# The down projection starts on the tokens' first half, operand sums are made in place, and layer normalization's reciprocals are pinned: one decoder layer in single precision

## The chip, the cores and the metric

The kernel runs on one core of a Trainium2 chip. The time is the device time of one execution in microseconds (us); for the kernel before it is the median of three runs, and the rows come from one further execution that the hardware profiler recorded. Engines: TensorE (PE) multiplies, VectorE (DVE), ScalarE (ACT) and GpSimd (POOL) do elementwise work, SyncE (SP) issues loads. POOL issues the DMAs that add to their destination.

## The reference, cut to what matters

One layer on 1024 tokens with 1024 channels, all in float32. The part that most of the change touches is the channel mixer's end:

```python
h = rmsnorm(x, g_ffn[i])
u = jnp.einsum("bsd,df->bsf", h, w_up[i])                      # 1024 -> 2 x 2816
f_gate = causal_dwconv(u[..., :D_FF], conv_f_w[i]) + conv_f_b[i]
f = jax.nn.gelu(f_gate, approximate=True) * u[..., D_FF:]
x = x + jnp.einsum("bsf,fd->bsd", f, w_down[i])                # 2816 -> 1024
pg = jax.nn.sigmoid(jnp.einsum("bsd,de->bse", rmsnorm(x, g_ple[i]), w_ple_gate[i]))
```

Before it stand an input projection (`w_in`, operand h), two convolution branches (one with a layer normalization over 512 channels), their merge, and an output projection; all are touched only through the operand sums and the normalization's two reciprocals.

## The kernel before

Channels lie on partitions (tiles of 128), tokens along the free dimension, 1024 of them in two halves `H0` and `H1` of 512. A float32 operand is held as two halves of its precision, `hi` (an ACT cast, L132) and `lo` (a DVE subtraction, L133), and one product of a weight block with an operand is three matmuls of 128x512 (hi·hi, hi·lo, lo·hi).

The large products are done in pairs: two row blocks of channels and the two token halves form a 2x2 block product, which class `Pair` (L607) computes with seven products m = 1 to 7 instead of eight. Products 1, 2 and 3 use operand rows as they are (`r1` and `r2` are the first token half of two feature tiles, `r3` the second half of the second tile); 4 to 7 use sums of them. `right_sums` (L583) makes these sums into two fresh tiles `t13` and `t24`, and `sum_halves` (L592) casts and subtracts them into hi and lo. Weight sums come from DMAs that add, issued on POOL (L244); `w_s` is a weight sum, `w_r` and `w_q` are plain weights.

The down projection works through 22 feature tiles in three chunks of 4, 4 and 3 rows (a row is a pair of tiles, k and 11+k). `f`, the product that the up projection left in DRAM (`f_d`), is loaded per chunk. A chunk has 28 steps (p, m): four pairs of output tiles p, seven products each; a step is 3 matmuls for each row, so 12 in the first two chunks and 9 in the last. The order of the steps, `dn_order`, is one list for all chunks: (0,1), (1,1), (0,2), (1,2), (0,6), ...; so four steps go by before the first sum is needed. `Rows.prepare` (L1108) is called after every step with the number of steps left before the chunk; it issues the loads (6 steps ahead for the first two rows of the first chunk, 3 for the other two, 14 elsewhere), the splits of plain operands and the sums (`Rows.sums`: rows 0 and 1 at two and one steps left, the others at none).

Results of the first two chunks are added to `x1_d` in DRAM by class `DnStore` (L1145) with DMAs of a full tile of 128x1024 (512 KB); the last chunk (`DnLast`, L1173) loads these tiles back (`x2`) and finishes them on DVE.

PE and SP run in the order of the code; the order on DVE, ACT and POOL is worked out by a scheduler, except for instructions given to `keep_in_program_order`. All three engines execute strictly in that order. `Loader` (L168) issues weights ahead by a distance in matmuls. Buffers are slots of one pool; the sums before take slots of their own.

## Time and profile before

| what | value |
|---|---|
| median of 3 runs | 1379.69 us (1376.6 to 1381.29) |
| profiled execution | 1382.37 us, of which the span (first to last instruction) is 1380.6 us |
| mean granted clock of TensorE | 0.972 |
| busy: PE / DVE / ACT / POOL | 1306.8 / 976.6 / 590.3 / 247.1 us |
| DMA moved | 245.25 MB |

The profile gives, for each stretch, how long an engine was busy and how many instructions it ran (x), the clock granted to TensorE (1.00 is 2.4 GHz, and 0.50 is 1.2 GHz), and the mean busy share of the 16 DMA engines. In full swing PE starts 90 matmuls of 128x512 in 20 us, so a stretch with fewer has lost the difference at 4.5 per us. PE's busy time hides this, since matmuls at the lower clock are busy for longer.

### The profile page before, as it was taken

The numbers are of one execution on the slowest core, as the hardware profiler recorded it, in microseconds if no ns is written. First come the engines' busy times: TensorE is split into PE (matmuls) and PEld (weight loads), VectorE is DVE, ScalarE is ACT, GpSimd is POOL, SyncE is SP. The second block draws the span as 40 slices with busy tenths as digits, with TensorE's granted clock in tenths as the row PEclk, the third lists the DMA queues.
The fourth block names the chain that finished last, engine by engine and source line by source line (L and its number), as shares of the span: only waits on it lengthen the run. The fifth ranks groups of instructions, "written<-read, shape, count | busy, mean of one in ns | idle before, by whom it ended". The sixth has DMA issues, their size and how long they took to land.

```text
span 1380.6 us, 15699 instructions
## 1 busy us (share of the span) xinstructions
PE 1306.8 (95%) x5798; PEld 1081.9 (78%) x5798; DVE 976.6 (71%) x1134; ACT 590.3 (43%) x814; POOL 247.1 (18%) x319
## 2 busy tenths in 40 slices
PE   9989999999999999899999999999976979989996
PEld 7768888788887788778888888888864867867996
DVE  7969999999448766486665566665676292588787
ACT  7443233233444334354344433444344262456554
POOL 1331221122100001122221222212112222320011
PEclk9989999999999999999999999999998999999998
DMA  9645696578676303597666776667666998994222
GB/s 339 183 119 125 179 237 159 142 200 212 196 272 233 122 24 130 163 205 189 177 167 175 198 186 172 174 168 192 187 181 162 272 222 204 211 234 153 76 91 73
DMA packets 102765, 245.25 MB, mean 178 GB/s; under 512 B 11680, under 2 KB 21664, under 8 KB 102688
## 3 DMA queue, kind: packets, MB, share of 16 engines
q1 hardware_dynamic: 61632, 148.81, 32.6%
q0 software_dynamic: 41056, 95.44, 32.1%
q8 instruction: 45, 0.74, 0.2%
q14 instruction: 32, 0.26, 0.1%
HBM read 173.42 MB, written 45.09 MB: 158 GB/s over the span
## 4 chain that ended last, share of the span: by engine, by line
PE 71%; DVE 14%; issue 8%; DMA 3%; ACT 2%; POOL 1%; SPq 0%; DVEq 0%; ACTq 0%; POOLq 0%
PE ps L629 50%; PE ps L155 14%; DVE acc L712 2%; PE ps L969 2%; PE ps L968 2%; PE ps L970 2%; DMA x_d<-dn 2%; DVE w_s_lo L133 1%; POOL s L244 1%; DMA f<-f_d 1%; DVE w_r_lo L133 1%; DVE x_raw L477 1%; DVE ft_lo L133 1%; DVE sc_cv L712 1%; DVE t L588 1%
## 5 line engine op out<-in xcount | busy, mean ns | idle before, releaser
L712 DVE SCALAR_TENSOR_TENSOR acc<-a,prm,acc 128x1023 f32<-128x1023 f32 (+14 forms) x120 | 151.8, 1265 | 1.7
L133 DVE TENSOR_TENSOR w_s_lo<-s,w_s_hi 128x1024 fp32r<-128x1024 f32 (+1 forms) x100 | 119.6, 1198 | 35.7 <-ACT w_s_hi L132 35.7
L244 POOL DMA_DIRECT2D s<-s x100 | 85.6, 856 | 298.2 <-DMA s<-s 126.0
L652 ACT COPY u<-ps 128x512 f32<-128x512 f32 x50 | 29.3, 586 | 202.3 <-PE ps L629 202.3
L132 ACT CAST w_s_hi<-s 128x1024 fp32r<-128x1024 f32 (+1 forms) x100 | 102.9, 1031 | 2.6 <-issue 1.7
L712 DVE SCALAR_TENSOR_TENSOR fg<-u_t,neg_f,fg 128x1023 f32<-128x1023 f32 (+1 forms) x44 | 56.5, 1283 | 28.3 <-ACT fg L706 27.6
L133 DVE TENSOR_TENSOR w_r_lo<-raw_r,w_r_hi 128x1024 fp32r<-128x1024 f32 (+1 forms) x50 | 59.8, 1197 | 17.2 <-ACT w_r_hi L132 17.2
L646 ACT COPY u<-ps 128x512 f32<-128x512 f32 x50 | 29.3, 586 | 92.4 <-PE ps L629 92.4
L629 PE MATMUL ps<-xgs_hi,w_s_lo 128*128 128x512 f32 x176 | 68.6, 390 | 0.0
L629 PE MATMUL ps<-xgs_lo,w_s_hi 128*128 128x512 f32 x176 | 68.5, 389 | 0.0
L629 PE MATMUL ps<-xgs_hi,w_s_hi 128*128 128x512 f32 x176 | 68.5, 389 | 0.0
L629 PE MATMUL ps<-xgp_hi,w_r_lo 128*128 128x512 f32 x176 | 68.5, 389 | 0.0
L629 PE MATMUL ps<-xgp_lo,w_r_hi 128*128 128x512 f32 x176 | 68.5, 389 | 0.0
L629 PE MATMUL ps<-xgp_hi,w_r_hi 128*128 128x512 f32 x176 | 68.5, 389 | 0.0
L639 ACT COPY ps<-ps 128x512 f32<-128x512 f32 x50 | 28.5, 571 | 87.6 <-PE ps L629 87.6
L1075 DVE TENSOR_TENSOR u_t<-ps,rstd 128x512 f32<-128x512 f32 x22 | 15.2, 691 | 69.7 <-PE ps L629 69.7
L155 PE MATMUL ps<-xp_hi,whi 128*128 128x448 f32 (+2 forms) x192 | 62.0, 323 | 1.9 <-DVE x L1201 1.9
L629 PE MATMUL ps<-xgq,w_s_hi 128*128 128x512 f32 x176 | 55.8, 399 | 7.2 <-DVE u_t L665 7.2
L155 PE MATMUL ps<-xp_lo,whi 128*128 128x448 f32 (+2 forms) x192 | 61.9, 323 | 0.0
L155 PE MATMUL ps<-xp_hi,wlo 128*128 128x448 f32 (+2 forms) x192 | 61.9, 323 | 0.0
L629 PE MATMUL ps<-xgt_hi,w_q 128*128 128x512 f32 x176 | 57.9, 390 | 0.7 <-ACT u L652 0.7
L629 PE MATMUL ps<-hss_hi,w_s_hi 128*128 128x512 f32 x128 | 50.9, 398 | 4.5 <-ACT w_s_hi L132 4.5
(297 smaller groups left out, 3718.7 us busy)
## 6 DMA issues: line engine op xcount, KB each, us to landing
s<-s POOLq DMA_DIRECT2D x92, 256.0 KB, 4.1
raw_r<-w_up SPq DMA_DIRECT2D x22, 512.0 KB, 4.7
s<-w_up SPq DMA_DIRECT2D x44, 256.0 KB, 3.0
s<-w_up SPq DMA_DIRECT2D x22, 512.0 KB, 5.8
s<-w_up POOLq DMA_DIRECT2D x44, 256.0 KB, 6.0
f_d<-v_t POOLq DMA_DIRECT2D x22, 512.0 KB, 5.9
f<-f_d SPq DMA_DIRECT2D x22, 512.0 KB, 9.8
s<-w_in SPq DMA_DIRECT2D x32, 256.0 KB, 3.2
```

The lines of the kernel that those rows point to most:

```text
L132: nc.scalar.copy(hi, src)
L133: nc.vector.tensor_sub(lo, src, f32(hi))
L155: nc.tensor.matmul(ps[:, :step], wt[:, b], xt[:, t : t + step], start=f, stop=l)
L244: nc.gpsimd.dma_start(dst, src, accum_op=ALU.add)
L629: nc.tensor.matmul(ps, wt[:, b], xt, start=f, stop=l, skip_group_check=True)
L639: nc.scalar.copy(self.b, self.a)
L646: nc.scalar.copy(self.e[:, H0], self.b)
L652: nc.scalar.copy(self.e[:, H1], self.b)
L712: nc.vector.scalar_tensor_tensor(dst[:, s:], src[:, : T - s], w(k), dst[:, s:], ALU.mult, ALU.add)
L968: nc.tensor.matmul(ps, whi[:, b], hi, start=first and k == ks[0], stop=False)
L969: nc.tensor.matmul(ps, whi[:, b], lo, start=False, stop=False)
L970: nc.tensor.matmul(ps, wlo[:, b], hi, start=False, stop=last and k == ks[-1])
```

## The change

It has five parts. (1) `dn_order` becomes a function of the chunk: the first eight steps of a chunk are now the products 1 and 2 of all four pairs, which need the first token half alone; the other steps follow in a new order. (2) `Rows` loads each pair of tiles by token halves (two DMAs of 256 KB into one tile, instead of one of 512 KB), and a table `STEPS` says at which step, counted from the chunk's first, each row is loaded, split and summed. (3) `right_sums` writes the sums over the tiles they are made of, for the input projection's h, the output projection's xg and for f. (4) `DnStore` adds each quarter (128x512, 256 KB) as soon as it is ready; `DnLast` loads its second tile at m = 6. (5) `ln_end` is split: the square roots and reciprocals (`ln_stats`) come first in the code, the gate multiplication after them is pinned behind them, and the rest of `ln_end` follows.

```diff
-        def right_sums(a0, a1, b0, b1, eng=nc.vector):
-            t13, t24 = slot("t13"), slot("t24")
-            eng.tensor_sub(t13[:, H0], a0, a1)
-            eng.tensor_sub(t13[:, H1], b1, a1)
...
+        def right_sums(a0, a1, b0, b1, eng=nc.vector):
+            eng.tensor_sub(a0, a0, a1)
+            eng.tensor_sub(a1, b1, a1)
+            nc.vector.scalar_tensor_tensor(b1, a0, -1.0, b1, ALU.mult, ALU.subtract)
+            nc.vector.scalar_tensor_tensor(b0, b1, -1.0, b0, ALU.mult, ALU.subtract)
...
+    def dn_order(ci):
+        if ci == 0:
+            order = [(p, m) for m in (1, 2) for p in range(4)]
+        else:
+            order = [(0, 1), (1, 1), (0, 2), (2, 1), (1, 2), (3, 1), (2, 2), (3, 2)]
+        order += [(0, 6), (0, 5), (0, 7)]
+        for p in (1, 2):
+            order += [(p, 6), (p - 1, 4), (p, 5), (p - 1, 3), (p, 7)]
...
-        def ln_end():
+        def ln_stats():
             for c in HALVES:
                 ps = bank()
                 cs_mm(ps, ones_c, cs, c)
                 sqrt(lr[:, c], ps)
+            for c in HALVES:
                 inverse(lr[:, c])
+        def ln_end():
             for c in range(KC):
                 nc.vector.tensor_mul(acc[c], acc[c], lr)
...
+                    first = jj == 2 and j == jj and c is H0
+                    ins = nc.vector.tensor_mul(g[:, c], ps, g[:, c])
+                    if first:
+                        tc.keep_in_program_order(ins)
                 t_t[j] = g
+            if jj == 2:
+                ln_end()
...
         def o_sums(i):
             x0, x1 = xg[i, 0], xg[i, HB]
-            rows[i].update(sum_halves(*right_sums(x0[:, H0], x1[:, H0], x0[:, H1], x1[:, H1]), "xg"))
-            rows[i][3] = half_split(x1[:, H1], "xgq")
+            r = rows[i]
+            r[3] = half_split(x1[:, H1], "xgq")
+            right_sums(x0[:, H0], x1[:, H0], x0[:, H1], x1[:, H1])
+            r[5], r[4], r[7], r[6] = sum_halves(x0, x1, "xgs")
...
+            STEPS = {
+                "load0": ((-8, -8, -8, -8), (-20, -19, -18, -17)),
+                "plain": ((-3, -3, -2, -2), (-12, -11, -10, -9)),
+                "load1": ((-2, -2, -2, -2), (-14, -13, -12, -11)),
+                "sums13": ((1, 1, 2, 2), (-8, -7, -6, -5)),
+                "sums24": ((2, 2, 3, 3), (-4, -3, -2, -1)),
+                "split23": ((3, 3, 4, 4), (0, 1, 2, 3)),
+                "split14": ((5, 5, 6, 6), (1, 2, 3, 4)),
+            }
...
+            def load(self, ci, i, c):
                 k = DROWS[ci][0] + i
-                self.raw[ci, i] = load(f_d[k], "f"), load(f_d[KH + k], "f")
+                t = slot("f")
+                nc.sync.dma_start(t[:, H0], f_d[k][:, c])
+                nc.sync.dma_start(t[:, H1], f_d[KH + k][:, c])
+                return t
...
-            def ready(self, i):
-                self.n[i] += 1
-                if self.n[i] == 2:
-                    nc.gpsimd.dma_start(x1_d[self.j + 4 * i], self.o[i], accum_op=ALU.add)
+            def add(self, i, c, o):
+                nc.gpsimd.dma_start(x1_d[self.j + 4 * i][:, c], o, accum_op=ALU.add)
...
+                if m == 6 and last:
+                    live[p].to.load(p + 4)
                 live[p].step(m)
-                if not last:
-                    f_rows.prepare(ci + 1, len(dn_order) - 1 - n)
+                f_rows.prepare(ci, n + 1)
+                f_rows.prepare(ci + 1, n + 1 - len(order))
```

The diff adds lines, so that L133 of before is L135 after, and L586 to L589 of before become L1154, L1155, L1160 and L1161 for f.

First place: DVE where the first chunk's sum products begin. In the names, `t` is a tile of sums, `fs` and `ft` are their halves, `f_q` a plain half, and `w_s` the first weight sum. Before, from the last row's sums to the weights:

```order
L133 TENSOR_TENSOR fs_lo<-t_7337,fs_hi 128x1024
L133 TENSOR_TENSOR ft_lo<-t_7338,ft_hi 128x1024
L133 TENSOR_TENSOR f_q<-f,f_q 128x512
L586 TENSOR_TENSOR t_7354<-f 128x512
L587 TENSOR_TENSOR t_7354<-f 128x512
L588 SCALAR_TENSOR_TENSOR t_7355<-t_7354,f 128x512
L589 SCALAR_TENSOR_TENSOR t_7355<-t_7355,f 128x512
L133 TENSOR_TENSOR fs_lo<-t_7354,fs_hi 128x1024
L133 TENSOR_TENSOR ft_lo<-t_7355,ft_hi 128x1024
L133 TENSOR_TENSOR f_q<-f,f_q 128x512
L133 TENSOR_TENSOR w_s_lo<-s_7100,w_s_hi 128x1024
L133 TENSOR_TENSOR w_s_lo<-s_7101,w_s_hi 128x1024
```

After, the same place (f_s are the halves of sums, made in f itself):

```order
L1161 SCALAR_TENSOR_TENSOR f<-f 128x512
L1160 SCALAR_TENSOR_TENSOR f<-f 128x512
L135 TENSOR_TENSOR f_s_lo<-f,f_s_hi 128x1024
L1161 SCALAR_TENSOR_TENSOR f<-f 128x512
L135 TENSOR_TENSOR f_s_lo<-f,f_s_hi 128x1024 x5
L135 TENSOR_TENSOR w_s_lo<-s_7173,w_s_hi 128x1024
L135 TENSOR_TENSOR f_s_lo<-f,f_s_hi 128x1024 x2
L135 TENSOR_TENSOR w_s_lo<-s_7174,w_s_hi 128x1024
L135 TENSOR_TENSOR w_s_lo<-s_7273,w_s_hi 128x1024
```

Before, sums and splits alternated row by row; now all sums stand ahead, then the splits, and the first `w_s` stands between the sixth and the seventh split.

Second place: DVE where the second chunk's sum products begin. Before:

```order
L586 TENSOR_TENSOR t_7978<-f 128x512
L587 TENSOR_TENSOR t_7978<-f 128x512
L588 SCALAR_TENSOR_TENSOR t_7979<-t_7978,f 128x512
L589 SCALAR_TENSOR_TENSOR t_7979<-t_7979,f 128x512
L133 TENSOR_TENSOR fs_lo<-t_7978,fs_hi 128x1024
L133 TENSOR_TENSOR ft_lo<-t_7979,ft_hi 128x1024
L133 TENSOR_TENSOR f_q<-f,f_q 128x512
L133 TENSOR_TENSOR w_s_lo<-s_7753,w_s_hi 128x1024
L133 TENSOR_TENSOR w_s_lo<-s_7754,w_s_hi 128x1024
```

After (L1223 is the last `dn` of the chunk before, which marks where its last product ended):

```order
L1223 TENSOR_TENSOR dn<-ps,u_7810 128x512
L1161 SCALAR_TENSOR_TENSOR f<-f 128x512
L135 TENSOR_TENSOR f_s_lo<-f,f_s_hi 128x1024
L135 TENSOR_TENSOR w_r_lo<-raw_r,w_r_hi 128x1024
L135 TENSOR_TENSOR f_s_lo<-f,f_s_hi 128x1024 x4
L135 TENSOR_TENSOR w_r_lo<-raw_r,w_r_hi 128x1024
L135 TENSOR_TENSOR f_s_lo<-f,f_s_hi 128x1024 x3
L135 TENSOR_TENSOR w_s_lo<-s_7856,w_s_hi 128x1024
```

The sums have gone ahead of the chunk's start, and eight splits and two plain weights are left between it and the first `w_s`.

Third place: DVE at the layer normalization, where `lrstd` is the row of reciprocals, `gate` a multiplication by a gate and `an_lo` the low half of the normalized operand. Before:

```order
L922 TENSOR_TENSOR gate<-ps,gate 128x512 x2
L133 TENSOR_TENSOR wlo<-raw,whi 128x1024
L922 TENSOR_TENSOR gate<-ps,gate 128x512 x2
L133 TENSOR_TENSOR wlo<-raw,whi 128x1024
L387 RECIPROCAL lrstd<-lrstd 128x512 x2
L922 TENSOR_TENSOR gate<-ps,gate 128x512
L912 TENSOR_TENSOR acc<-acc,lrstd 128x1024 x4
L922 TENSOR_TENSOR gate<-ps,gate 128x512 x3
L133 TENSOR_TENSOR an_lo<-acc,an_hi 128x1024 x4
```

After:

```order
L940 TENSOR_TENSOR gate<-ps,gate 128x512
L135 TENSOR_TENSOR wlo<-raw,whi 128x1024
L940 TENSOR_TENSOR gate<-ps,gate 128x512 x2
L135 TENSOR_TENSOR wlo<-raw,whi 128x1024
L403 RECIPROCAL lrstd<-lrstd 128x512 x2
L940 TENSOR_TENSOR gate<-ps,gate 128x512
L929 TENSOR_TENSOR acc<-acc,lrstd 128x1024 x4
L940 TENSOR_TENSOR gate<-ps,gate 128x512 x3
L135 TENSOR_TENSOR an_lo<-acc,an_hi 128x1024
L940 TENSOR_TENSOR gate<-ps,gate 128x512
L135 TENSOR_TENSOR an_lo<-acc,an_hi 128x1024 x3
```

Ahead of the reciprocals one gate fewer is left; the two gates and the weight split right ahead of them stand as before.

## Rows read from the trace of the kernel before

**Rows 1.** The page: busy us (share of the span) x instructions.

```profile
PE 1306.8 (95%) x5798; PEld 1081.9 (78%) x5798; DVE 976.6 (71%) x1134; ACT 590.3 (43%) x814; POOL 247.1 (18%) x319
```

**Rows 2.** Windows: us, then PE, PEld, DVE, ACT, POOL, PEclk, DMA share, GB/s.

```profile
980.00:1000.00 20.00, 20.00 (x90) 16.57 (x89) 12.77 (x15) 7.87 (x10) 3.15 (x4) 1.00 0.82 263
1000.00:1060.00 60.00, 39.43 (x149) 30.47 (x147) 44.58 (x57) 27.84 (x38) 8.80 (x11) 0.83 0.65 175
1060.00:1120.00 60.00, 59.75 (x262) 49.15 (x263) 27.06 (x34) 24.78 (x37) 15.49 (x18) 1.00 0.95 234
1120.00:1160.00 40.00, 31.15 (x124) 24.40 (x123) 26.55 (x33) 18.99 (x25) 8.63 (x10) 0.87 0.79 189
1160.00:1200.00 40.00, 40.00 (x178) 33.14 (x177) 12.19 (x16) 15.15 (x24) 9.48 (x11) 1.00 0.99 236
1200.00:1240.00 40.00, 33.88 (x138) 26.32 (x137) 35.90 (x50) 22.90 (x35) 11.25 (x13) 0.91 0.90 228
```

**Rows 3.** Timeline of PE: start, us, instruction [idle before, releaser].

```profile
1018.82 1.22 PE L629 MATMUL ps<-xgq,w_s_hi 128*128 128x512 f32 x2 [7.17 <-DVE u_t L665]
...
1047.45 0.79 PE L629 MATMUL ps<-ft_hi,w_s_hi 128*128 128x512 f32 x1 [11.96 <-ACT w_s_hi L132]
...
1051.28 0.63 PE L629 MATMUL ps<-ft_lo,w_s_hi 128*128 128x512 f32 x1
1051.70 0.63 PE L629 MATMUL ps<-ft_hi,w_s_lo 128*128 128x512 f32 x1
```

**Rows 4.** Chain of waits ahead of the first stall: start, us, what.

```profile
1003.70 11.62 DMA f<-f_d
```

**Rows 5.** Timeline of DVE, end of the second stall.

```profile
1042.23 0.69 DVE L586 TENSOR_TENSOR t<-f 128x512 f32<-128x512 f32 x1
1042.84 0.68 DVE L587 TENSOR_TENSOR t<-f 128x512 f32<-128x512 f32 x1
...
1044.77 1.22 DVE L133 TENSOR_TENSOR fs_lo<-t,fs_hi 128x1024 fp32r<-128x1024 f32 x1
1045.96 1.23 DVE L133 TENSOR_TENSOR ft_lo<-t,ft_hi 128x1024 fp32r<-128x1024 f32 x1
...
1047.70 2.37 DVE L133 TENSOR_TENSOR w_s_lo<-s,w_s_hi 128x1024 fp32r<-128x1024 f32 x2
```

**Rows 6.** DMA, 1000 to 1240 us: queues (packets, MB, share), issues (KB, median us).

```profile
q0 software_dynamic: 9072, 20.25, 47.4%
q1 hardware_dynamic: 14204, 30.33, 37.0%
...
f<-f_d SPq DMA_DIRECT2D x18, 512.0 KB, 10.4
x_d<-dn POOLq DMA_DIRECT2D x16, 512.0 KB, 8.5
s<-w_dn SPq DMA_DIRECT2D x28, 256.0 KB, 4.6
s<-s POOLq DMA_DIRECT2D x15, 256.0 KB, 5.0
```

**Rows 7.** Timeline of SP's DMA issues: start, us.

```profile
1062.99 11.52 SPq L856 DMA_DIRECT2D f<-f_d  x8
```

**Rows 8.** Timeline of POOL, DVE and PE at the input sums.

```profile
59.56 1.61 POOL L586 TENSOR_TENSOR t<-x_raw 128x512 f32<-128x512 f32 x1
...
59.46 5.97 DVE L477 SCALAR_TENSOR_TENSOR x_raw<-x_raw,prm,rstd 128x512 f32<-128x512 f32 x1
...
66.09 0.50 PE L155 MATMUL ps<-h_lo,whi 128*128 128x512 f32 x1 [2.12 <-DVE h_lo L482]
```

**Rows 9.** Timeline of DVE at the normalization and at the output sums.

```profile
436.01 6.56 DVE L387 RECIPROCAL lrstd<-lrstd 128x512 f32<-128x512 f32 x2
...
602.90 1.23 DVE L133 TENSOR_TENSOR cs_lo<-sq,cs_hi 128x1024 fp32r<-128x1024 f32 x1 [1.11 <-ACT cs_hi L132]
```

**Rows 10.** Waits of PE, 425 to 460 us: us in total, times, longest.

```profile
PE ps L155 <- ACT an_hi L132: 2.9, 1, 2.9
```

More of the change, by code (lines that the diff above doesn't have):

```diff
@@ L351, in trunk_kernel @@
     ld.add_pairs("up", [(w_up[KF + j], w_up[j]) for j in range(KF)], up_order)
[L352 removed]
     for ci, (k0, n) in enumerate(DROWS):
[L354 removed]
+        pairs = [(w_dn[j], w_dn[KD // 2 + j]) for j in range(KD // 2)]
+        ld.add_pairs(("dn", ci), pairs, dn_order(ci), k0, KH + k0, n)
     for j in range(KD):
@@ L1099, in plain @@
-            def plain(self, ci, i):
-                a, b = self.raw[ci, i]
-                r = self.rows[ci][i]
-                r[1], r[2] = half_split(a[:, H0], "f_q"), half_split(b[:, H0], "f_q")
-            def sums(self, ci, i):
-                a, b = self.raw[ci, i]
-                r = self.rows[ci][i]
-                r.update(sum_halves(*right_sums(a[:, H0], a[:, H1], b[:, H0], b[:, H1]), "f"))
-                r[3] = half_split(b[:, H1], "f_q")
-            def prepare(self, ci, left):
-                n = DROWS[ci][1]
-                if left == (6 if ci == 0 else 14):
-                    for i in range(2 if ci == 0 else n):
-                        self.load(ci, i)
-                if left == 5:
-                    for i in range(2 if ci == 0 else n):
-                        self.plain(ci, i)
-                if left == 3 and ci == 0:
-                    for i in range(2, n):
-                        self.load(ci, i)
-                        self.plain(ci, i)
-                if left == 2:
-                    self.sums(ci, 0)
-                if left == 1:
-                    self.sums(ci, 1)
-                if left == 0:
-                    for i in range(2, n):
-                        self.sums(ci, i)
@@ new lines, in halves, with split23, split14, prepare @@
+            def halves(self, ci, i, t, ma, mb):
+                hi, lo = split(t, "f_s")
+                r = self.rows[ci][i]
+                r[ma], r[mb] = (hi[:, H0], lo[:, H0]), (hi[:, H1], lo[:, H1])
+            def split23(self, ci, i):
+                self.halves(ci, i, self.s1[ci, i], 7, 6)
+            def split14(self, ci, i):
+                self.halves(ci, i, self.s0[ci, i], 5, 4)
+            def prepare(self, ci, t):
+                if ci < len(DROWS):
+                    for step, at in self.STEPS.items():
+                        for i in range(DROWS[ci][1]):
+                            if at[min(ci, 1)][i] == t:
+                                getattr(self, step)(ci, i)
@@ L1175, in __init__, with load @@
                 self.j = j
-                for k in (j, j + 4):
-                    x1[k] = load(x1_d[k], "x2")
-                    xg2[k] = (slot("xp_hi", F32R), slot("xp_lo", F32R))
+                self.load(j)
+            def load(self, k):
+                x1[k] = load(x1_d[k], "x2")
+                xg2[k] = (slot("xp_hi", F32R), slot("xp_lo", F32R))
             def ready(self, k, c):
```

89 lines of the change are left out of this document (56 added, 33 removed).

## The prediction

> **What bounds the kernel now.** I read the page first: PE is busy 95% of the span [rows 1], so time can come only from PE's starts being late or slow, since the number of matmuls stays 5798. Busy time can't show that, so next I read windows and counted starts. A stretch at full speed has 90 starts in 20 us, 4.5 per us (the window at 980 of [rows 2]). Against that the three chunk starts of the down projection fall short: 149 of 270 at 1000 to 1060, 124 of 180 at 1120 to 1160, 138 of 180 at 1200 to 1240 [rows 2]. The shortfalls of 121, 56 and 42 starts are 26.9, 12.4 and 9.3 us, 48.6 together; between them (1060 to 1120, 1160 to 1200) 10 starts lack, 2.2 us. The granted clock is 1.00 in these two and 0.83, 0.87 and 0.91 in the three, so part of the loss is clock that follows on a stall.
>
> Then the timeline of PE says what the first loss consists of: 7.17 us before 1018.82, 11.96 us before 1047.45, and starts 0.42 us apart behind it (the level of 1.2 GHz) against 20/90 = 0.222 us [rows 3]. The chain of waits gives the first stall its cause: a load of `f` that took 11.62 us [rows 4]; its casts and subtractions stand on DVE ahead of the `u_t` that frees PE's bank. The second has DVE as its cause, although its row names an ACT cast: ACT runs in order, and the cast of `w_s` stands behind casts of sums that DVE was still making and splitting until 1045.96; `w_s_lo` follows at 1047.70 [rows 5]. DVE is busy 44.58 of 60 us there, but 12 to 27 of 40 to 60 between the chunks [rows 2]: it has room, in another place.
>
> **The sum, part by part.** All is set against the profiled execution, 1382.37 us, which stands 2.7 above the median of 1379.69; I take 2.7 off at the end.
>
> *First chunk.* Removed: the stall of 7.17. The first halves are now loaded eight up-projection steps before the chunk. A step is 12 matmuls, 2.67 us, so 21.3 us pass before the chunk starts, and the plain splits (three and two steps ahead) come 13.3 us or more after the issue; the load that was late took 11.62 [rows 4]. Moved: eight steps, 96 matmuls or 21.3 us (four before, 10.7), run before a sum is needed. In that time DVE must do, behind the up projection's tail: the tail itself (after the last product two products by `rstd`, four operations of 1024 columns, two of `fg`, and a wait for the activation that I estimate as one more of them: 2x0.61 + 7x1.19 = 9.5), then 16 sum operations and 4 plain splits at 0.61 from start to start, six sum splits and one `w_s` at 1.19 [rows 5]: 12.2 + 8.3 = 20.5. The first `w_s` stands behind the sixth split (first place in the order), so it ends 30.0 us after the up projection, and PE stands still from 21.3 on: a stall of 8.7. The second halves' loads, issued two steps before the chunk, land 11.62 - 5.3 = 6.3 us into it, before DVE's tail is done at 9.5, so they are hidden; without this cover each us of lateness costs one. Behind the stall I put 3 us of slow starts, as before (15 starts 0.2 too far apart). Loss 11.7 instead of 26.9: gain 15.2. Bounds: if ACT and DVE alternate as badly as before, 11.96 + 3 is lost still and the gain is 11.9; if DVE's tail overlaps the last steps, 21.
>
> *Second and third chunk.* Sums move ahead of the chunk's start. At the second start DVE has left, behind the previous chunk's last `dn`: one sum, eight splits, two plain weights, and then `w_s` (second place in the order): 0.6 + 11x1.19 = 13.7 us, against 21.3 of plain products. At the third, by the same count, it is five splits, a plain weight, the `w_s` and four short operations, 7x1.19 + 4x0.61 = 10.8 at most, against 8 x 9 matmuls = 16 us. Neither stall should stay. The operations that moved ahead (some 20 of 0.61 for each chunk) lie in stretches where DVE was busy 27.06 of 60 and 12.19 of 40 us [rows 2]. Gain 12.4 + 9.3, of which I keep back 2 for small waits: 19.7. Bounds: 10 if `w_s` at the third start is late by the old amount, 23.9 if the 2.2 between the chunks goes as well.
>
> *Loads and stores.* New on SP are 22 issues of 256 KB (44 in place of 22), new on POOL 16. Their bytes are the same. But 0.65x60 + 0.95x60 + 0.79x40 + 0.99x40 + 0.90x40 = 203 us of mean DMA busy time [rows 2] must now fit into 240 - 34.9 = 205 us. PE ran at 1.00 with shares of 0.95 and 0.99, so this is near the edge and not over it; at an average share of 0.97 the stage takes 209 to 210. I charge 5. Bounds: 0 (the first halves' 2 MB go ahead of 1000 us, where the share is 0.82), and 22 (below, first rival). As to each smaller transfer, rows show 256 KB landing in 4.6 against 10.4 for 512 KB from SP, and 5.0 against 8.5 for adding ones [rows 6], and eight whole loads issued in one stretch of 11.52 us [rows 7]; so I charge a half-load as half. The Trainium skill says otherwise (DMA: Bandwidth & Descriptors, section Anatomy of one DMA — SWDGE (gpsimd) path): a DMA costs about 2.0 us fixed plus bytes over 436 GB/s, which makes 256 KB 2.6 us and 512 KB 3.2. By it the 16 additional stores alone would cost an estimated 32 us, were they done one after another; the medians above, where half the bytes take 0.44 and 0.59 of the time, do not bear out a fixed part of that weight in a loaded queue.
>
> *Input sums.* A subtraction on POOL takes 1.61, and beside the first four of them one DVE operation stood 5.97 us in place of about 0.7; PE idled 2.12 behind it [rows 8]. In place, all eight subtractions can follow one another without waiting for slots, and DVE's half of the sums may start earlier. What the pairing then costs no row shows: from -5.3 (one more such operation) to +5 (the wait of 2.12, the clock after it). I take +2, near the row of the wait.
>
> *Output sums.* All four sums and a plain split go ahead of the first cast; the chain to `cs_lo` at 602.90 [rows 9] is one operation longer: -0.6, bounds -1.2 and 0.
>
> *Normalization.* The two reciprocals take 6.56 [rows 9], PE waits 2.9 for what follows [rows 10]. The order shows them behind the same two gates and weight split, with one gate moved past them: 0, bounds -0.6 and +2.9.
>
> Sum: 15.2 + 19.7 - 5 + 2 - 0.6 + 0 = 31.3; 1382.4 - 31.3 = 1351.1 profiled, 1348 on the runs' basis.
>
> **Rivals.**
> 1. *The DMA engines become the bound.* For: 203 us of transfers in 205; POOL issues adding DMAs strictly in order, so that stores that wait for a result hold up weight sums behind them. Against: 60 us at 0.95 with PE at 262 starts [rows 2]. Were 0.90 (the share at 1200) the most that lasts, the stage takes 226 us, not 205: 21 in place of the 5 charged, and the time is 1364.
> 2. *The first chunk's stall stays as it was and one of the two others comes back,* because the splits, now bunched behind all sums, alternate between ACT and DVE: gain 11.9 + 10 in place of 34.9, so 13 less: 1361.
> 3. *Slower: a transfer costs by its number, not by its bytes.* Place: the down projection's f loads and adding stores. The loads are 18 x 0.524 = 9.4 of 30.33 MB on a queue with 37.0% of 240 us: 27.6 us; the stores 16 x 0.524 = 8.4 of 20.25 MB at 47.4%: 47 us [rows 6]. If a half costs as much as a whole, 75 us are added to 203, and the stage takes 278 even at a share of 1.0: 38 longer than now, so about 1416. It decides for the worse once 203 + x is over 240, that is once a half costs over 0.75 of a whole. Against it: 0.44 and 0.59 [rows 6], though these are of other tensors; at 0.59 the stores alone would add 8.
>
> **How the numbers follow.** Forecast 0.57 (own range 1336 to 1357), rival 1 0.18, rival 2 0.13, rival 3 0.09 (half of it between no change and +10 us), 0.03 for a better end (1330, with the input sums at +5 and the losses of the chunks all gone). The range 1334 to 1367 holds the forecast with rivals 1 and 2. What can be told from no change is 0.3%, 4 us: faster 0.88 (the first two rivals too, but for 0.03 of theirs that ends worse than its price), same 0.04, slower 0.08.
>
> **What would show it.** Right: no PE idle on `u_t` at the end of the up projection; one PE idle of about 8 us before the first chunk's ninth step, released by `w_s`; over 85 starts in every 20 us at both later chunk starts; DMA share about 0.95 through the stage; reciprocals still right behind the two gates. Wrong: PE idle on `w_r` or `w_s` whose own load had just landed (rivals 1 and 3; median landing of a half-load over 7.8 us, 0.75 of 10.4, would be rival 3); a stall of 12 us or more in the first chunk (rival 2); PE idle near 60 to 100 us longer than before.

## The result and the profile after

| | before | after |
|---|---|---|
| median of the runs compared | 1378.14 us (4 runs, 1376.37 to 1381.29) | 1359.72 us (4 runs, 1355.46 to 1361.27) |
| ratio after/before, 95% interval | | 0.9859 [0.9827, 0.9891] |
| profiled execution | 1382.37 us | 1361.27 us |

The change makes the kernel faster by 18.4 us in the medians (1.4%) and 21.1 in the profiled executions. The forecast was 1348, a gain of 31.3; the time lies inside the range (1334 to 1367), and a third of the expected gain did not come. Rows are those of one execution of each kernel, which can stand some 5 us off the median of its runs.

The page of the kernel after, answering to [rows 1]: PE's busy time is nearly the old one, so the gain is idle time and clock.

```profile
PE 1303.0 (96%) x5798; PEld 1079.8 (79%) x5798; DVE 977.9 (72%) x1134; ACT 588.5 (43%) x814; POOL 260.8 (19%) x335
```

Windows of the kernel after, with the columns of [rows 2]. The first three lie outside the down projection; the five others are its stage, in which the chunks now start near 1020, 1100 and 1187.

```profile
60.00:100.00 40.00, 31.57 (x115) 24.68 (x114) 30.03 (x28) 15.25 (x19) 12.81 (x12) 0.83 0.45 101
440.00:460.00 20.00, 15.33 (x58) 11.71 (x58) 17.38 (x17) 10.32 (x10) 0.00 (x0) 0.83 0.31 106
560.00:620.00 60.00, 53.01 (x211) 41.96 (x210) 39.58 (x40) 24.89 (x30) 14.86 (x19) 0.91 0.76 190
1000.00:1060.00 60.00, 51.75 (x207) 40.17 (x206) 48.39 (x59) 31.93 (x44) 16.09 (x20) 0.91 0.92 255
1060.00:1120.00 60.00, 60.00 (x267) 49.69 (x266) 43.87 (x57) 33.12 (x48) 18.25 (x22) 1.00 0.94 211
1120.00:1180.00 60.00, 60.00 (x266) 49.70 (x265) 31.61 (x42) 24.70 (x38) 21.68 (x25) 1.00 1.00 238
1180.00:1220.00 40.00, 32.45 (x132) 26.02 (x131) 23.65 (x30) 20.19 (x30) 13.09 (x15) 0.91 1.00 248
1220.00:1260.00 40.00, 36.96 (x163) 30.03 (x162) 34.62 (x53) 26.67 (x45) 1.71 (x2) 1.00 0.48 148
```

PE's starts, at 4.5 per us, give back the whole difference. First chunk start: 63 of 270 lack, 14.0 us, against 26.9 before, so 12.9 won. Second start and all to 1180: 7 of 540 lack, 1.6 us, against 12.4 + 2.2, so 13.0 won. Third start: 48 of 180 lack, 10.7 us, against 9.3, so 1.4 lost. In the first three windows the kernel before had 125, 52 and 223 starts: 2.2 lost, 1.3 won, 2.7 lost. The sum is 20.9 of the 21.1 measured. So two chunk starts did what was forecast, the third did not, and the input sums cost instead of gaining. The first three windows are not firm: kernels below with the same code there and the same lead of weights have 118 to 134, 52 to 54 and 220 to 221 starts, where this one has 115, 58 and 211.

The timeline of PE after (start, duration, instruction, [idle before <- releaser]) shows the starts that answer to [rows 3], and [rows 8] for the input sums:

```profile
68.57 0.79 PE L157 MATMUL ps<-h_lo,whi 128*128 128x512 f32 x1 [5.14 <-DVE h_lo L498]
...
1022.46 0.73 PE L642 MATMUL ps<-f,w_r_hi 128*128 128x512 f32 x2 [1.62 <-ACT w_r_hi L132]
1023.72 0.50 PE L642 MATMUL ps<-f,w_r_lo 128*128 128x512 f32 x1 [0.53 <-DVE w_r_lo L135]
...
1027.37 0.50 PE L642 MATMUL ps<-f,w_r_lo 128*128 128x512 f32 x1 [0.64 <-DVE w_r_lo L135]
...
1046.64 0.79 PE L642 MATMUL ps<-f_s_hi,w_s_hi 128*128 128x512 f32 x1 [2.89 <-ACT w_s_hi L132]
...
1050.30 0.80 PE L642 MATMUL ps<-f_s_hi,w_s_lo 128*128 128x512 f32 x1 [2.44 <-DVE w_s_lo L135]
...
1055.16 0.63 PE L642 MATMUL ps<-f_s_lo,w_s_hi 128*128 128x512 f32 x1
1055.59 0.63 PE L642 MATMUL ps<-f_s_hi,w_s_lo 128*128 128x512 f32 x1
...
1200.83 0.72 PE L642 MATMUL ps<-f,w_r_hi 128*128 128x512 f32 x2 [2.98 <-ACT ps L652]
...
1211.84 0.80 PE L642 MATMUL ps<-f_s_hi,w_s_hi 128*128 128x512 f32 x1 [4.58 <-ACT u L659]
```

The wait on `u_t` of 7.17 is gone, and the 11.96 for the first `w_s` have become 2.89 + 2.44. The two waits at 1200 and 1211 name ACT copies (L652 and L659, PE's partial results): what held ACT is the question of the third start.

Its answer stands in four timelines of the kernel after. ACT (a square sum waits for a store, then a cast for DVE's addition to a loaded `x`) and that addition on DVE:

```profile
1198.00 0.63 ACT L434 ACTIVATE ssq<-x 128x512 f32<-128x512 f32 x1 [5.02 <-DMA x_d<-dn]
...
1209.66 0.72 ACT L1247 ACTIVATE xp_hi<-x,prm 128x512 fp32r<-128x512 f32 x1 [4.10 <-DVE x L1253]
```

```profile
1208.94 0.69 DVE L1253 TENSOR_TENSOR x<-ps,x 128x512 f32<-128x512 f32 x1 [5.38 <-DMA x<-x_d]
```

SP (the third and fourth load of `x`, of which the fourth stands till 1204.6; the next weights follow it) and, below, two such loads of the kernel before, which do not stand:

```profile
1187.33 17.64 SPq L870 DMA_DIRECT2D x<-x_d  x2
1205.38 0.33 SPq L242 DMA_DIRECT2D s<-w_dn  x1
```

```profile
1203.69 1.75 SPq L856 DMA_DIRECT2D x<-x_d  x2
```

POOL (weight sums `s<-w_dn` and `s<-s`, and the adding stores `x_d<-dn` of the second chunk, in one queue):

```profile
1182.79 2.08 POOL L246 DMA_DIRECT2D s<-w_dn  x2
1189.86 0.86 POOL L246 DMA_DIRECT2D s<-s  x1 [4.98 <-DMA s<-w_dn]
1191.40 0.86 POOL L246 DMA_DIRECT2D s<-s  x1 [0.69 <-issue]
1191.94 1.20 POOL L1209 DMA_DIRECT2D x_d<-dn  x1
1196.96 0.85 POOL L246 DMA_DIRECT2D s<-s  x1 [3.83 <-DMA s<-s]
1197.50 2.08 POOL L1209 DMA_DIRECT2D x_d<-dn  x2
```

DVE wrote the last `dn` of that chunk at 1184.34, for 0.68 us. Its store is issued at 1197.88, behind three weight sums of which two waited for DMAs, and takes 6.45 more. ACT's square sum stands behind the store ahead of it (issued at 1191.94): it has no part in that store's data, so it must want the slot. SP's load wants either a slot or the data that the third chunk loads back; PE comes to a stop behind both. The experiments take slot and data apart.

### The profile page after: what moved, and what is told of

Read it like the earlier page. It is cut to its first block, busy times and chain, and to the rows that moved or that the text cites. A ratio compares the mean times of both kernels' runs of the same rounds, so it can differ in the third digit from the quotient of the medians.

```text
span 1359.5 us, 15764 instructions
## 1 busy us (share of the span) xinstructions
PE 1303.0 (96%) x5798; PEld 1079.8 (79%) x5798; DVE 977.9 (72%) x1134; ACT 588.5 (43%) x814; POOL 260.8 (19%) x335
## 4 chain that ended last, share of the span: by engine, by line
PE 76%; DVE 13%; DMA 4%; issue 4%; ACT 2%; POOL 0%; SPq 0%; DVEq 0%; ACTq 0%; POOLq 0%
PE ps L642 54%; PE ps L157 15%; DVE acc L725 2%; PE ps L992 2%; PE ps L991 2%; PE ps L990 2%; DMA x_d<-dn 2%; DMA s<-w_dn 1%; DVE w_s_lo L135 1%; DVE x_raw L493 1%; DVE ssq L442 1%; DMA x<-x_d 1%; DVE sc_cv L725 1%; DVE rstd L403 0%; DVE lrstd L403 0%
## 5 line engine op out<-in xcount | busy, mean ns | idle before, releaser
L135 DVE TENSOR_TENSOR w_s_lo<-s,w_s_hi 128x1024 fp32r<-128x1024 f32 (+1 forms) x100 | 119.5, 1199 | 29.0 <-ACT w_s_hi L132 29.0
L642 PE MATMUL ps<-xgs_hi,w_s_hi 128*128 128x512 f32 x264 | 103.0, 390 | 0.0
L642 PE MATMUL ps<-xgs_hi,w_s_lo 128*128 128x512 f32 x264 | 102.9, 390 | 0.0
L642 PE MATMUL ps<-xgs_lo,w_s_hi 128*128 128x512 f32 x264 | 102.9, 390 | 0.0
L642 PE MATMUL ps<-hs_hi,w_s_lo 128*128 128x512 f32 x192 | 76.7, 400 | 3.8 <-DVE w_s_lo L135 3.8
L642 PE MATMUL ps<-hs_hi,w_s_hi 128*128 128x512 f32 x192 | 76.2, 397 | 2.6 <-ACT w_s_hi L132 2.6
L642 PE MATMUL ps<-hs_lo,w_s_hi 128*128 128x512 f32 x192 | 75.9, 395 | 0.0
L659 ACT COPY u<-ps 128x512 f32<-128x512 f32 x50 | 29.3, 587 | 85.4 <-PE ps L642 85.4
L1099 DVE TENSOR_TENSOR u_t<-ps,rstd 128x512 f32<-128x512 f32 x22 | 15.2, 692 | 69.7 <-PE ps L642 69.7
L652 ACT COPY ps<-ps 128x512 f32<-128x512 f32 x50 | 28.6, 571 | 84.6 <-PE ps L642 84.6
L135 DVE TENSOR_TENSOR w_r_lo<-raw_r,w_r_hi 128x1024 fp32r<-128x1024 f32 (+1 forms) x50 | 59.8, 1197 | 5.5 <-ACT w_r_hi L132 5.4
L642 PE MATMUL ps<-f_s_hi,w_s_hi 128*128 128x512 f32 x132 | 54.2, 411 | 8.7 <-ACT u L659 5.8
```

Of the source, the lines that this page charges most:

```text
L135: nc.vector.tensor_sub(lo, src, f32(hi))
L642: nc.tensor.matmul(ps, wt[:, b], xt, start=f, stop=l, skip_group_check=True)
L652: nc.scalar.copy(self.b, self.a)
L659: nc.scalar.copy(self.e[:, H0], self.b)
```

## The experiments

Each ratio is to the kernel before; the changed kernel's is 0.9859, or 1359.72 us.

**The third chunk's loads of x without their data chain.** The tiles are loaded from the layer's input, so the result leaves out what the first two chunks added.

```
-                x1[k] = load(x1_d[k], "x2")
+                x1[k] = load(xT[k * P : (k + 1) * P], "x2")
```

> The changed kernel, but the last chunk loads its x2 tiles from the input x and not from the tensor to which the chunks before add; so the first two chunks' contribution is left out of the output. Theory A (the stall left at the third chunk's start, 48 of 180 starts short in 1180 to 1220, is the chain store to DRAM, load of x2, addition on DVE, casts on ACT that stand ahead of the copies PE waits for): the two waits of PE at 1200.8 and 1211.8 (2.98 and 4.58) go, with the slow starts behind them; 7 to 10 us less than the changed kernel, about 1351. Rival B (ACT and DVE are simply too full there, or the DMA engines at a share of 1.0 hold weights up): the waits stay, under 3 us of gain, 1357 or more.

Measured: 0.9843 [0.9819, 0.9867], 1359.7 us. The waits stay (4.61 and 3.52 us), 1180 to 1220 has 120 starts, and SP still stands before the fourth load, though its source is never written:

```profile
1181.48 24.35 SPq L870 DMA_DIRECT2D x<-xT  x2
```

So the data alone are not what the load waits for: without them it still stands for a store, by the slot, out of a pool of 54 that all tiles of this size share.

**Input sums on DVE instead of POOL.**

```
-            right_sums(xa[:, H0], xa[:, H1], xb[:, H0], xb[:, H1], nc.gpsimd)
+            right_sums(xa[:, H0], xa[:, H1], xb[:, H0], xb[:, H1])
```

> The changed kernel with the input projection's eight subtractions on DVE and not on POOL. Theory A (DVE's operation of 7.17 us at 60.7 stands because POOL works through subtractions of SBUF tiles at that time): no operation of DVE there over 1.5 us, PE's wait of 5.14 on h_lo gone, 60 to 100 us short by fewer than 55 starts in place of 63; DVE works 5 us more, so 1 to 5 us less in all, about 1357. Rival B (DVE is the bound of that stretch, and its own 5 us of additional work come on top): equal or up to 4 us slower, 1360 to 1364.

Measured: 0.9805 [0.9781, 0.9829], 1353.65 us, with 141 starts at 60 to 100 against 115. First the changed kernel's POOL and, below, its DVE in that stretch (timelines):

```profile
60.87 2.84 POOL L609 TENSOR_TENSOR x_raw<-x_raw 128x512 f32<-128x512 f32 x2
63.37 2.77 POOL L610 TENSOR_TENSOR x_raw<-x_raw 128x512 f32<-128x512 f32 x2
65.81 1.54 POOL L609 TENSOR_TENSOR x_raw<-x_raw 128x512 f32<-128x512 f32 x1
```

```profile
60.73 7.17 DVE L493 SCALAR_TENSOR_TENSOR x_raw<-x_raw,prm,rstd 128x512 f32<-128x512 f32 x1
```

and DVE of the experiment, the same operation at the same place:

```profile
60.76 0.73 DVE L493 SCALAR_TENSOR_TENSOR x_raw<-x_raw,prm,rstd 128x512 f32<-128x512 f32 x1
```

The operation stands through five POOL subtractions and takes 0.73 without them; PE's 5.14 for `h_lo` is gone. The 26 starts are 5.8 us, and the medians differ by 6.1.

The same subtractions on POOL need not cost this. Of the kernels below that leave them there and in place, four hold one DVE operation 7.09 to 7.34 us, like this one, and have 119 to 121 starts in the window; in two (both chains cut, and weight sums later everywhere) DVE and POOL meet a little otherwise, no DVE operation takes over 2.31 and 2.19, and there are 134 and 141 starts, where the kernel before has 125. So what POOL costs here hangs on how the two series fall against each other. In the kernel with the weight sums later DVE gets in between the subtractions (POOL first, then DVE):

```profile
58.27 3.44 POOL L609 TENSOR_TENSOR x_raw<-x_raw 128x512 f32<-128x512 f32 x2
61.66 3.41 POOL L610 TENSOR_TENSOR x_raw<-x_raw 128x512 f32<-128x512 f32 x2
```

```profile
62.18 1.75 DVE L498 TENSOR_TENSOR h_lo<-x_raw,h_hi 128x512 fp32r<-128x512 f32 x1
63.85 1.77 DVE L493 SCALAR_TENSOR_TENSOR x_raw<-x_raw,prm,rstd 128x512 f32<-128x512 f32 x1
```

**The down projection's part alone.** Input and output sums made in tiles of their own again, normalization as before.

```
-            right_sums(xa[:, H0], xa[:, H1], xb[:, H0], xb[:, H1], nc.gpsimd)
-            r[5], r[7], r[4], r[6] = sum_halves(xa, xb, "hs")
+            r.update(fresh_halves(*fresh_sums(xa[:, H0], xa[:, H1], xb[:, H0], xb[:, H1], nc.gpsimd), "hs"))
...
+            r.update(fresh_halves(*fresh_sums(x0[:, H0], x1[:, H0], x0[:, H1], x1[:, H1]), "xg"))
             r[3] = half_split(x1[:, H1], "xgq")
-            right_sums(x0[:, H0], x1[:, H0], x0[:, H1], x1[:, H1])
-            r[5], r[4], r[7], r[6] = sum_halves(x0, x1, "xgs")
...
-        def ln_stats():
+        def ln_end():
...
-            for c in HALVES:
                 inverse(lr[:, c])
-
-        def ln_end():
...
-                    if first:
-                        tc.keep_in_program_order(ins)
```

> The changed kernel with the parts outside the down projection as before: input and output sums in fresh tiles, normalization without the pin. Theory A (starts lost by window: in-place sums cost 2 us at 60 to 100 and 2.5 at 560 to 620, the pin gives 1.3): 3 us less than the changed kernel, about 1356.5. Rival B (these windows only shift losses; the three parts are neutral together): within 1.5 us of it. Rival C (they help, as the prediction had it for the input sums): 1 to 3 us more.

Measured: 0.9815 [0.9791, 0.9839], 1355.24 us. So all that the change does outside the down projection costs some 4 to 6 us, and the windows say where: 131 starts at 60 to 100, 59 and 213 in the two others, where the changed kernel has 115, 58 and 211. So it is the input sums in the main; the windows show no cost of the normalization or of the output sums.

**Two plain products of the third chunk moved behind its first sum products.** The loads of `x` for pairs 2 and 3 are issued right before these products.

```
+        if ci == len(DROWS) - 1:
+            order = order[:6] + [(0, 6), (2, 2), (0, 5), (3, 2), (0, 7)]
...
-                self.load(j)
+                if j < 2:
+                    self.load(j)
...
+                if last and (p, m) in ((2, 2), (3, 2)):
+                    live[p].to.load(p)
```

> The changed kernel, but in the third chunk products (2,2) and (3,2), which need the x2 tiles, come after (0,6) and (0,5), and these two loads are issued right ahead of them. Theory A (the chain of store, x2 load and consumer is late by some 10 us): the stall of 4.58 shrinks and the one of 2.98 goes; 4 to 8 us less, about 1354. Rival B (the sums for (0,6) are now needed two steps, 4 us, earlier, and DVE is late with them): no gain or up to 4 us slower, 1360 to 1364.

Measured: 0.9913 [0.9891, 0.9936], 1368.24 us, slower than the changed kernel. The waits on ACT's copies shrink to 3.2 in all, but PE now waits 7.2 for `w_r_lo` and 5.6 for `w_q`, weights that stand behind the moved loads; 109 starts at 1180 to 1220, 138 at 1220 to 1260. It is slower than the rival had it, and not for the rival's cause, late sums.

**Both chains cut.** As the first experiment (the same contribution is left out), and `dn` gets eight half tiles of its own; the shared pool shrinks from 54 to 50 to make room.

```
-NBIG = 54
+NBIG = 50
...
+    dnp = ctx.enter_context(tc.tile_pool(name="dnp", bufs=8))
...
-                t = DnStore.part
-                DnStore.part = slot("dn") if t is None else None
-                return DnStore.part[:, H0] if t is None else t[:, H1]
+                return dnp.tile([P, HB], F32, tag="dn", name="dn")
...
-                x1[k] = load(x1_d[k], "x2")
+                x1[k] = load(xT[k * P : (k + 1) * P], "x2")
```

> The changed kernel with x2 loaded from the input x as in e1 (the first two chunks' contribution is left out of the output) and, besides, the 128x512 results of DnStore in a pool of their own (8 of them), with 50 and not 54 slots left in the common pool. In e1 SP's x2 load still waited 24 us, for a store: the slot that it takes was one of `dn`, and so was that of the first square sum on ACT. Theory A (stores that land late hold the third start, through their data and through their slots): with both cut, PE's waits on L652 and L659 there (4.6 and 3.5 in e1) go, and 1180 to 1220 has at least 160 starts; 6 to 9 us less than the changed kernel, ratio 0.980 to 0.981. Rival B (DMA engines at a share of 1.0 hold it whatever the chain): waits of the same length on weights; ratio 0.985 or more.

Measured: 0.9885 [0.9859, 0.9911], 1363.65 us. The windows of this kernel from 1120 on:

```profile
1120.00:1180.00 60.00, 55.12 (x237) 45.18 (x236) 26.32 (x36) 22.68 (x36) 20.99 (x24) 0.97 0.96 223
1180.00:1220.00 40.00, 40.00 (x178) 33.14 (x177) 32.15 (x44) 24.45 (x38) 13.60 (x16) 1.00 0.99 254
1220.00:1260.00 40.00, 33.80 (x139) 27.38 (x139) 30.83 (x45) 23.79 (x37) 1.20 (x2) 0.91 0.44 138
```

At 1180 to 1220 the loss is gone, 178 starts at a granted clock of 1.00. But 29 starts are lost ahead of it and 24 behind it, in waits of 4.9 and 4.6 us on ACT's copies at places that had none. 46 were won and 53 lost. The fourth load of `x` now goes at 1191.7, not 1204.6:

```profile
1185.80 6.22 SPq L871 DMA_DIRECT2D x<-xT  x2
```

**`dn` in a pool of its own, nothing left out.** Four half tiles; the shared pool has 52.

```
-NBIG = 54
+NBIG = 52
...
+    dnp = ctx.enter_context(tc.tile_pool(name="dnp", bufs=4))
```

> The changed kernel with the results of DnStore in a pool of their own (4 of 128x512), 52 slots in the common pool, and nothing left out. Theory A1 (the slot is what holds: x2 and square sums wait for a store only because they get its slot): like e5, ratio about 0.980. Theory A2 (the data hold: x2 must wait for the store to land anyhow): the square sum's wait goes, the x2 wait stays; 2 to 4 us gain, ratio 0.983 to 0.985.

Measured: 0.9858 [0.9834, 0.9882], 1359.64 us, the changed kernel's time. 149 starts at 1180 to 1220 (17 won), 243 at 1120 to 1180 (23 lost). ACT's square sum no longer waits, and PE's first wait of this start is gone; but SP still stands before the fourth load, now for the data alone, and PE waits 3.41 behind it:

```profile
1184.30 18.25 SPq L871 DMA_DIRECT2D x<-x_d  x2
```

With the changed kernel and the two that load `x` from the input, this one makes a table of starts lacking of 180: 48 with both chains, 60 without the data, 31 without the slots of `dn`, 2 without either. Each chain is enough to hold the load. The pool had 4 or 2 slots fewer in two of these kernels, and whether the starts lost elsewhere come from that was not tried.

**Weight sums issued later, everywhere.**

```
-AHEAD = {"whole": 150, "r": 110, "q": 100, "s": 150, "late": 200}
+AHEAD = {"whole": 150, "r": 110, "q": 100, "s": 120, "late": 200}
```

> The changed kernel with weight sums issued 120 and not 150 matmuls ahead. POOL issues in order, and the last stores of the second chunk, whose data are ready at 1184, are issued at 1191.9 and 1197.5 behind weight sums of the third chunk that wait for their loads. Theory A (that order delays the stores): the stores are issued within 4 us of their data, the third start loses under 25 starts, ratio 0.980 to 0.983, unless weight sums come late elsewhere. Rival B (30 matmuls, 7 us, are what the sums need): PE waits for w_s in the up projection, over 3 us in all, ratio 0.986 or more.

Measured: 0.991 [0.9887, 0.9932], 1367.59 us. The third start has 176 of 180 starts, with the data chain and the 54 slots left as they were. Elsewhere sums now come late: 236 starts at 1120 to 1180 (a wait of 4.8), 143 at 1220 to 1260, 186 at 560 to 620. These losses may be what cleared the third start: the second chunk's last `dn` comes at 1189.89, 5.6 us later than in the changed kernel, while the fourth load of `x` still waits 12.2 for a store and goes at 1204.04, hardly earlier than 1204.6. So this run does not show what POOL's order alone is worth.

**First chunk with half its sums.** Eight operations (L1160 and L1161) of the first chunk are left out, so products 4 to 7 of that chunk don't have their operands.

```
+                if ci == 0:
+                    return
                 nc.vector.scalar_tensor_tensor(v[:, H1], t[:, H0], -1.0, v[:, H1], ALU.mult, ALU.subtract)
```

> The changed kernel with the eight operations L1160 and L1161 of the first chunk left out (products 4 to 7 of that chunk use unfinished sums, so the output is not the reference's). Theory A (DVE's list of sums and splits sets the first start's stall, as the prediction has it): eight operations of 0.60 are 4.8 us less on DVE, and the waits of 2.89 and 2.44 at 1046.6 and 1050.3 go but for 0.5; with less slow clock behind them 5 to 8 us less, ratio 0.980 to 0.982. Rival B (ACT's casts and copies, or the loads of the second halves, set it): under 2 us less, 0.9845 or more.

Measured: 0.9833 [0.9809, 0.9857], 1356.23 us. The first start has 240 starts instead of 207, and the waits of 2.89 and 2.44 become none and 1.28: so the stall there is DVE's list of sums and splits. Of these 33 starts, 7.3 us, only 3.5 reach the median: 252 and 252 starts in the two windows from 1060 to 1180, where 267 and 266 were, take 29 of them back, and the third start has 10 more (142).

**The loads of `x` in halves,** on top of the input sums on DVE; the second halves are loaded behind the step with m = 6.

```
-                x1[k] = load(x1_d[k], "x2")
+                x1[k] = slot("x2")
+                nc.sync.dma_start(x1[k][:, H0], x1_d[k][:, H0])
...
+            def rest(self, k):
+                nc.sync.dma_start(x1[k][:, H1], x1_d[k][:, H1])
...
+                if last and m == 6:
+                    live[p].to.rest(p)
+                    live[p].to.rest(p + 4)
```

> The kernel of e2 (input subtractions on DVE), with the x2 tiles loaded by token halves: the first half, which product 2 needs and whose last addition in DRAM is many steps old, at the same place, the second half behind product 6. The loads then take slots whose former tiles are not results on their way to DRAM. Theory A (at the third start SP and DVE wait for stores of the second chunk's last steps, by data and by slot together): SP's x2 loads no longer stand 15 us or more, PE's wait on L659 there (3.5 to 4.6 before) is under 1 us, that on L652 (2.3 in e2, from a square sum whose slot still waits for a store) stays; 3 to 6 us less than e2's 1353.65, about 1349. Rival B (in that stretch any relief only lets another tile wait for a slot, as in e5 to e7): within 2 us of e2.

Measured: 0.9817 [0.9799, 0.9835], 1354.9 us, not to be told from the 0.9805 without it. That is the rival's outcome. The loads of `x` no longer stand for a store, but the next weight's load does (SP's waits from 1170 to 1225: us in total, times, longest), and ACT's wait of 5.05 for a store stays; the last two windows have 144 and 146 starts where they had 136 and 169.

```profile
SPq L242 <- DMA x_d<-dn: 17.5, 1, 17.5
```

That load reads a weight, so only a slot can tie it to the store.

**The old order in the second and third chunk.**

```
+        elif True:
+            return block_order(KD // 2, 2)
```

> The changed kernel with the second and third chunk in the order of steps of the kernel before (four steps ahead of the first sum, not eight), and the sums still made at the changed kernel's steps, ahead of the chunk. It tells what the order alone is worth. Theory A (it is the early sums that free the starts; by the prediction's count DVE has 13.7 us left at the second start against 10.7 in four steps, and 10.8 against 8.0 at the third): PE waits 3 us at the second start, and the third start is no worse than in the changed kernel, since x2 is consumed by fewer pairs early; within 4 us of the changed kernel, ratio 0.984 to 0.989. Rival B (the eight plain steps are what hides the sums): second start loses 8 us or more, ratio 0.991 or more.

Measured: 0.9902 [0.9884, 0.992], 1365.51 us. PE waits 3.2 at the second start (245 starts at 1060 to 1120) and 5.1 at the third (128 at 1180 to 1220). So the order is worth 5.8 us in the medians, between what the two theories had. The second start still lacks 25 of 270 where the kernel before lacked 56 of 180: the rest of what was won there must be of the early sums and the half-loads, which were not tried apart.

**A weight ahead of the last splits,** on top of the input sums on DVE and the loads in halves: in the first chunk four plain splits move one step back.

```
-                "split14": ((5, 5, 6, 6), (1, 2, 3, 4)),
+                "split14": ((6, 6, 7, 7), (1, 2, 3, 4)),
```

> The kernel of e9 with the splits for products 5 and 4 of the first chunk one step later, so that on DVE the first weight sum stands behind four sum splits instead of six. Theory A (DVE's list sets the first start's stall): two splits of 1.15 us fewer ahead of the weight, the stall (5.3 in two waits) shrinks by 2 to 2.5, and 1 more of slow clock at most; 2 to 3 us less than e9. Rival B (ACT's casts, which come in the same order, or the next products 5, which now wait for the splits, take it back): within 1 us of e9.

Measured: 0.9799 [0.9776, 0.9822], 1352.88 us. 219 starts at the first chunk against 207 there before; the waits are 0.51 and 3.04, 1.7 less in all. The time is the lowest so far, but its interval holds the 0.9805 and 0.9817 of the two kernels under it.

**Weight sums later in the third chunk alone,** on top of the last one.

```
+    def lead(kind, key):
+        return 120 if kind == "s" and key[0] == ("dn", 2) else AHEAD[kind]
...
-            self.loads.sort(key=lambda x: self.cost[x[0]] - AHEAD[x[1]])
+            self.loads.sort(key=lambda x: self.cost[x[0]] - lead(x[1], x[2]))
...
```

> One edit on top of the kernel with the weight ahead of the splits (ratio 0.9799): the loads and the weight sums of the third chunk alone are issued 120 matmuls ahead of their use instead of 150, so that on GpSimd's queue eight stores of the second chunk stand in one row where seven stood, and the last two stores stand behind fewer weight sums (the earlier run with 120 everywhere had 176 of 180 starts at the third start, but lost elsewhere). Theory A (at the third start, ScalarE and SyncE wait for stores that stand behind weight sums in GpSimd's order, and for the slots that early weight sums hold): the waits of 5.1 and 3.9 us there shrink to 4 together, 165 starts or more at 1180 to 1220, and the time is 3 to 7 us lower, ratio 0.975 to 0.978. Theory B (the chunk's own weight chain leaves no room: load, adding load and two sums take 6.4 + 8.2 + 2 x 5.9 = 26.4 us against 120 x 0.222 = 26.6): the third start's first waits go, but the weights' tiles come late behind it, at 1200 to 1260 as many starts are lost as are won, and the time is within 3 us of that kernel's, ratio 0.978 to 0.982.

Measured: 0.98 [0.9779, 0.982], 1352.62 us: the time of the kernel it stands on. The first wait changes its name. PE without the edit, and with it, where the lines stand 3 lower (timelines):

```profile
1192.26 0.73 PE L642 MATMUL ps<-f,w_r_hi 128*128 128x512 f32 x2 [3.89 <-ACT ps L652]
```

```profile
1195.08 0.51 PE L645 MATMUL ps<-f_s_hi,w_s_hi 128*128 128x512 f32 x1 [2.13 <-ACT u L662]
...
1208.97 0.50 PE L645 MATMUL ps<-f_s_hi,w_s_hi 128*128 128x512 f32 x1 [1.01 <-ACT u L662]
...
1231.63 0.80 PE L645 MATMUL ps<-f_s_hi,w_s_hi 128*128 128x512 f32 x1 [4.83 <-ACT u L662]
```

and ACT, now held by a weight sum where it was held 5.94 by a store:

```profile
1192.16 0.84 ACT L132 CAST w_s_hi<-s 128x768 fp32r<-128x768 f32 x1 [2.79 <-DMA s<-s]
```

The count at 1180 to 1220 is 146 against 147. This is the second theory's outcome, and the first wait is as it had it: with sums later the sum is what comes late, with sums earlier the store. SP is not freed: it still stands 15.2 for a store, 17.8 without the edit. The wait of 4.83 behind 1230 was 5.15 without the edit.

## Why the prediction was partly right

*First chunk: right.* Predicted was a loss of 11.7 in place of 26.9; it is 14.0. The first cause went as said: no PE wait on `u_t`. The second was put at one stall of about 8.7 in front of the first `w_s` and 3 of slow starts. The rows show 2.89 + 2.44 of stall, and 2.8 of smaller waits for plain weights (1.62 + 0.53 + 0.64) that the sum left out. Counted from start to start, against 0.222 apart, the two stalls cost 6.3, and the waits for weights between 1020 and 1031, with the slow starts behind each, 4.2. Behind the stall the starts stand some 0.43 apart until 1056.4, which costs 3.0 more, as put. The window that holds the stall:

```profile
1040.00:1060.00 20.00, 14.66 (x49) 11.01 (x48) 14.79 (x15) 11.18 (x14) 7.18 (x9) 0.74 0.99 285
```

PE is busy 14.66 of 20 us and starts 49 matmuls of 90, at a granted clock of 0.74. The cause of the stall is DVE's list, as the half list showed. Too high was the stall (8.7 for 6.3), and the plain weights' 4.2 were not in the sum; that the two partly cancel is luck.

*Second chunk: right.* 12.4 was to go and did, and with it most of the 2.2 between the chunks, which the sum had only in its bound. The order of steps is worth 5.8 in the medians; the rest must be of early sums and half-loads, untried apart.

*Third chunk: here the prediction failed,* in the sentence "Neither stall should stay". It counted DVE's operations, 10.8 us against 16, and that was no bound: the waits that decide are of other engines. The third chunk's tiles of `x` and its first square sum take slots that stores of the second chunk still hold, and these stores stand in POOL's one queue behind weight sums, many of which wait for another sum's DMA of 5 to 8 us (rows below). That it is not the data alone, the unchained load showed (120 of 180), and that it is not the slots alone, `dn` in its own pool (149); with both chains cut the loss went (178). No kernel turned this into a gain clear of the noise: in three that had more starts there (both chains cut, `dn` in its own pool, all weight sums later) as many were lost elsewhere, perhaps by the edits themselves, and in the three with the loads of `x` in halves SP still stands 15 to 18 us for a store. The 9.3 that were to go and the 1.4 lost besides are the 10.7 of this start. What POOL's order is worth stays open: no kernel here has moved the stores past the weight sums without delaying these, and an order of POOL with stores first and sums as early as now wasn't tried.

*Loads and stores: no such charge seen.* 5 us were kept for the DMA engines. At shares of 0.94 and 1.00 PE had 267 and 266 of 270 starts, so these engines are not the bound there. Rival 1 is wrong as it was priced, though its remark on POOL's strict order came true the other way round: not sums behind stores, but stores behind sums. Rival 3's mark was a half-load landing in over 7.8 us; it landed in 7.0. These are the issues of the kernel after, 1000 to 1240 us:

```profile
f<-f_d SPq DMA_DIRECT2D x36, 256.0 KB, 7.0
...
x_d<-dn POOLq DMA_DIRECT2D x32, 256.0 KB, 6.5
s<-w_dn POOLq DMA_DIRECT2D x16, 256.0 KB, 8.2
s<-s POOLq DMA_DIRECT2D x16, 256.0 KB, 5.1
```

The first two rows are the half-load and the half-store: half the bytes take 0.67 and 0.76 of [rows 6], more than the 0.44 and 0.59 taken for them, which were of other tensors. The load is under the 0.75 from which that rival decides, the store just over it.

*Rival 2: its number, not its mechanism.* It said 1361 with the first stall unchanged. The first stall went, and the third returned for a cause that it does not name.

*Input sums: wrong in sign.* +2 was taken from bounds of -5.3 to +5; the loss is 2.2 in this execution, and 0.9 to 2.2 over the kernels with the same hold. The lower bound had named the mechanism, one more DVE operation held by POOL: with eight subtractions free to follow one another, one operation was held 7.17 in place of 5.97 [rows 8] and PE 5.14 in place of 2.12. Taken was the row of the wait, as if the wait were to go. That it isn't bound to happen, the two kernels with 134 and 141 starts show. The Trainium skill (SBUF — State Buffer, sections Who interferes with whom and Summary: rules for kernel authors) says that a DVE instruction with two inputs in SBUF contends with a GpSimd instruction that reads SBUF, and that the one which comes second is blocked until the other ends. The rows agree in kind where DVE got in between (1.75 and 1.77 beside POOL's 1.7 each); but in the changed kernel the DVE operation stood through five such instructions, not one, though its row begins first, at 60.73 against 60.87.

*Output sums and normalization: right.* -0.6 was charged; the profiled run has 12 starts fewer at 560 to 620, 2.7 us, but the kernels with the same output sums and the same weight lead have 219 to 221 of the 223 before, under 1 us, and the one with the output sums of before has 213: so the 2.7 is not theirs. 440 to 460 has 52 starts before and 52 to 58 with the change, 59 with the normalization of before, so the 1.3 is not of the pin either. The reciprocals stand behind the gates as the order said:

```profile
436.71 1.22 DVE L135 TENSOR_TENSOR wlo<-raw,whi 128x1024 fp32r<-128x1024 f32 x1
437.84 6.56 DVE L403 RECIPROCAL lrstd<-lrstd 128x512 f32<-128x512 f32 x2
```

Against the sum, then: 12.9 for 15.2 at the first start (-2.3), 13.0 - 1.4 for 19.7 at the two others (-8.1), no DMA charge (+5), -2.2 for +2 at the input sums (-4.2), -2.7 for -0.6 in the window of the output sums (-2.1) and 1.3 for 0 in that of the normalization. Together -10.4; 31.3 - 21.1 is 10.2. The step that failed is the third start, with the input sums next. That no DMA charge came (+5) made up for half of what the chunk starts missed.

## What to carry to other kernels

Counting the work of the busy engine tells whether a stall can go, not whether it will: for every tile that a chunk allocates at its start, ask whose slot it takes and what frees it, and follow that through the queue which issues the release. Where stores and weight sums share one queue, moving either ahead can delay the other: here a wait changed its name and the time stayed. Where a tile waits for a slot and for data, taking away one of the two need not help. And an elementwise series on GpSimd is not free while VectorE is on PE's path; what it costs hangs on how the two fall against each other (7.17 us for one operation, or 1.75 each).

## What the runs showed of the hardware that was not expected

One DVE operation of 0.73 us stood 7.17 us beside five back-to-back POOL subtractions, while in another kernel the two engines took turns beside the same subtractions, 1.75 us for a DVE operation. A load of 256 KB took 7.0 us where 512 KB had taken 10.4, and an adding store 6.5 against 8.5, so half the bytes took clearly more than half the time to land. And PE kept 266 of 270 starts where the DMA engines were busy 1.00 of the time: a full queue of transfers by itself cost it nothing.
